# Two first gate blocks kept raw until the branch stage, other buffers for four weight loads, and a last gate pair in written order

## The chip, the cores and the metric

The program runs on one core of a Trainium2 chip. The metric is the time of one execution in microseconds of the device; lower is better. A core has a matrix engine (PE, with its weight loads shown apart as PEld), a vector engine (DVE), a scalar engine (ACT), a general engine (POOL), and a queue engine (SP) that issues transfers; ACT and POOL issue a few transfers of their own.

## The reference, cut to what matters

One encoder layer over 1024 tokens of width 1024: one input projection, two branches (neighbourhood attention and a gated linear recurrence), a gated merge, an output projection and an MLP. The change lies around the merge:

```python
(q_na, k_na, v_na, q_hg, z_f, z_b, i_hg, g_hg, gate_na, gate_hg) = split_cols(a @ w_in[l])
...
mix = jax.nn.sigmoid(gate_na) * y_na + jax.nn.sigmoid(gate_hg) * y_hg
h = h + mix @ w_o[l]
```

`y_na` and `y_hg` are the two branches' outputs after their own projections `w_na_out` and `w_hg_out`. The two gates have 2048 columns together; each is a product of the normalised input `a` with a slice of `w_in`.

## The kernel before, in words

Every matrix operand is float32 and is split into a high and a low part (`split`, lines 95 to 97: ACT casts the high part, DVE subtracts it from the source to get the low part). A product is three multiplies of 512 columns per 128 rows of depth: high by high, high by low, low by high. A `chain` (line 874) is such a product over half of the depth: 12 multiplies.

**Gates.** The gate columns are taken as 16 blocks of 128 columns in 8 pairs. The product of a pair with the input is done by a Winograd-like scheme with seven half products in place of eight. One of them, `g1[m]`, and the first half of the even block are computed early, in `first_gates` (line 903), two pairs at a time: four chains, then ACT copies the first product to `g1` (line 912) and takes the sigmoid of the second (`gate_out`, line 900) and writes it to DRAM (`gsp`, line 901). Those of pairs 0 to 3 are spread by the scheduler as filler through the last neighbourhood attention stage, which itself uses `Exp` on ACT (line 807), transposes on PE (lines 820 and 822, tile `ppt`), and on ACT and DVE takes the transposed scores apart again (lines 831 and 832, tile `PT`).

The rest is `gate_pair` (line 964), eight times. On PE, pair m issues the chains s4 (into bank `pc`), then the last chain of the pair before (a22, into that pair's `pb`), then s2 (into `pb`), s1 (adds into `pc`), s3 (adds into `pb`). DVE reads `pb` after s2 (line 972), `pc` after s1 (line 974), `pb` after s3 (line 977); POOL subtracts (line 978), DVE adds (line 979); the last chain's result is read at line 984. As s3 and a22 add into the bank that lines 972 and 977 read, PE may start s3 only when line 972 is done, and a22 only when line 977 is done. Weights of a pair come by two loads of 512 KB (line 953) into `raw` tiles, Winograd sums on DVE (lines 869 to 872) and five splits.

**Buffers.** `raw`, `hi` and `lo` tiles of 512 KB come from a pool `wp` with two buffers each; a second pool `gp` in the gate stage has two more of each. Pairs with odd m take `raw` from `wp`, even ones from `gp`.

**Branch stage** (line 1020 on). `branch_operand(br)` loads a branch's output from DRAM (`osp`) in four pieces of 512 KB (k = 0 to 3) through `raw` tiles of `wp`, and splits each piece into the operand tiles `o` (line 1018). For each pair of output columns the weights `w_hg` (then `w_na`) are loaded through the same two `raw` buffers (line 1025) and split; each product takes 12 multiplies (lines 122 to 124) into one of five banks, and DVE multiplies it by the gate `sg`, loaded from `gsp` (lines 1032, 1041, 1043, 1044).

**What sets the order.** The program is written in the order of the source and a list scheduler then reorders instructions on each engine as it expects them to be ready; each engine, and each queue, works through its list strictly in order. A stretch under `tc.manual_schedule` keeps the written order on the engines that it names.

Of the kernel before, what the change touches and what calls it, by code (L numbers as in the profile page):

```python
# [9 lines left out]
F32 = mybir.dt.float32  # L10
# [8 lines left out]
P = 128  # L19
# [29 lines left out]
def layer(ctx: ExitStack, tc: tile.TileContext, x, meta, w_in, w_na, w_hg, w_o, w_up, w_dn,  # L49
# [55 lines left out]
    def load_block(src, kc, scale=None, raw=None):  # L105

        if raw is None:
            raw = load_raw(src, kc)
        hi = wp.tile([P, KC, P], F32R, tag="hi", name="hi")
        lo = wp.tile([P, KC, P], F32R, tag="lo", name="lo")  # L110
        if scale is None:
            act.copy(hi[:, :kc], raw[:, :kc])  # L112
            dve.tensor_tensor(lo[:, :kc], raw[:, :kc], hi[:, :kc].bitcast(F32), op=ALU.subtract)  # L113
# [16 lines left out]
    def u_tiles(h, name):  # L130
        return [up.tile([P, KC, UW[h]], F32R, tag=f"u{h}{i}", name=f"{name}{h}{i}") for i in range(2)]
# [760 lines left out]
    def gate_col(c):  # L892
        return (C_GH if c < KC else C_GN) + (c % KC) * P
# [4 lines left out]
    def gate_out(c, h, t, src):  # L898

        act.activation(t, src, AF.Sigmoid)  # L900
        act.dma_start(gsp[c][:, h * TH:(h + 1) * TH], t)

    def first_gates(ms):

        blocks, ps = [], []
        for m in ms:
            hi, lo = load_block(w_in[:, gate_col(2 * m):gate_col(2 * m) + P], KC)
            blocks.append([[flat(t)[:, q * TH:(q + 1) * TH] for t in (hi, lo)] for q in range(2)])
        for m, b in zip(ms, blocks):
            ps.append(mm_tile())  # L910
            chain(ps[-1], b[0], aV["b11"], True)
            act.copy(g1[m], ps[-1])
        for m, b, p in zip(ms, blocks, ps):
            chain(p, b[1], aV["b21"], False)
            gate_out(2 * m, 0, gfp.tile([P, TH], F32, tag="go", name="go", bufs=2), p)

    psum_pools(pa=2, pb=2, pc=2)
    first_gates((0, 1))
# [27 lines left out]
    def gate_sums(m):  # L946

        raw = []
        for q in range(2):
            t = (wp.tile([P, KC, P], F32, tag="raw", name="raw") if m % 2 else  # L950
                 gp.tile([P, KC, P], F32, tag="raw", name="raw", bufs=2))
            c = gate_col(2 * m + q)
            sp.dma_start(t, w_in[:, c:c + P].rearrange("(k p) c -> p k c", p=P))
            raw.append(flat(t))
        sa, sb = g_tile("sx", D, bufs=2), g_tile("sx", D, bufs=2)
        winograd(dve, raw[0][:, :TH], raw[0][:, TH:], raw[1][:, :TH], raw[1][:, TH:],
                 sb[:, :TH], sa[:, TH:], sb[:, TH:], sa[:, :TH])
        W = {}
        W["s4"], W["s2"] = gate_weights(sa)
        W["s1"], W["s3"] = gate_weights(sb)  # L960
        W["a22"], = gate_weights(raw[1][:, TH:])
        return W

    def gate_pair(m, W, before):
        pb, pc = up_bank("pb"), up_bank("pc")
        p3 = gpr.tile([P, TH], F32, tag="p3", name="p3", bufs=2)
        chain(pc, W["s4"], aV["b22"], True)
        act.copy(p3, pc)
        before()
        chain(pb, W["s2"], aV["t2"], True)  # L970
        u1, u3, u2 = (g_tile("gv", TH, bufs=5) for _ in range(3))
        dve.tensor_tensor(u1, pb, g1[m], op=ALU.add)
        chain(pc, W["s1"], aV["t1"], False)
        dve.tensor_tensor(u1, u1, pc, op=ALU.add)
        gate_out(2 * m, 1, u1, u1)
        chain(pb, W["s3"], aV["t3"], False)
        dve.tensor_tensor(u3, pb, g1[m], op=ALU.add)
        pool.tensor_tensor(u3, u3, p3, op=ALU.subtract)
        dve.tensor_tensor(u3, u3, pc, op=ALU.add)
        gate_out(2 * m + 1, 1, u3, u3)  # L980

        def last():
            chain(pb, W["a22"], aV["t4"], False)
            dve.tensor_tensor(u2, pb, g1[m], op=ALU.add)
            gate_out(2 * m + 1, 0, u2, u2)
        return last

    first_gates((4, 5))
    first_gates((6, 7))
    W = gate_sums(0)  # L990
    for v in ("t2", "t1", "t3", "t4"):
        second_operand(v)
    last = lambda: None
    for m in range(NG):
        last = gate_pair(m, W, last)
        if m + 1 < NG:
            W = gate_sums(m + 1)
    last()
    gps.close()
    gfs.close()  # L1000

# [9 lines left out]
    osrc = [u_tiles(br, "o") for br in range(2)]  # L1011
    mix = [mixp.tile([P, KC, TH], F32, name=f"mix{h}") for h in (1, 0)][::-1]

    def branch_operand(br):
        for k in range(4):
            raw = wp.tile([P, KC, P], F32, tag="raw", name="raw")
            sp.dma_start(flat(raw), osp[br][k])
            split(*(t[:, 2 * k:2 * k + 2, :TH] for t in osrc[br]), raw.rearrange("p (h a) b -> p h (a b)", h=2))

    branch_operand(0)  # L1020
    for br, wsrc in enumerate((w_hg, w_na)):
        for jj in range(0, KC, 2):
            raw, hi, lo = (flat(wp.tile([P, KC, P], dt, tag=t, name=t))
                           for t, dt in (("raw", F32), ("hi", F32R), ("lo", F32R)))
            sp.dma_start(raw.rearrange("p (k c) -> p k c", k=4),
                         wsrc[:, jj * P:(jj + 2) * P].rearrange("(k p) c -> p k c", p=P))
            split(hi, lo, raw)
            if br == 0 and jj == 2:
                branch_operand(1)
            for j in (jj, jj + 1):  # L1030
                sg = sgp.tile([P, T], F32, tag="sg", name="sg")
                sp.dma_start(sg, gsp[8 * br + j])
                for h in range(2):
                    pm = mm_tile()
                    t = slice(h * TH, (h + 1) * TH)
                    for k in range(4):
                        c = slice(k * 2 * P + (j - jj) * P, k * 2 * P + (j - jj + 1) * P)
                        sh, sl = (o[:, 2 * k + h, :TH] for o in osrc[br])
                        mm3(pm, hi[:, c], lo[:, c], sh, sl, k == 0, k == 3)
                    if br == 0:  # L1040
                        dve.tensor_tensor(mix[h][:, j], pm, sg[:, t], op=ALU.mult)
# [608 lines left out]
```

## Time and profile before

| | |
|---|---|
| median of 3 runs | 1529.9 us (1528.22 to 1530.62) |
| the profiled execution, its own time | 1530.97 us |
| its span, first to last instruction | 1529.2 us (1.77 us lie around it) |
| PE busy | 1503.1 us, 98% of the span |
| DVE, ACT, POOL busy | 68%, 43%, 25% |
| mean granted PE clock | 0.997 |

A row of the timeline has the start in us, the duration in us, the engine, the source line, the operation, out<-in tiles, shape, and in brackets how long the engine sat idle before it and what ended that. A row of the waits has the engine and line that waited, who released it, and the total, the number of times and the longest. A row of the windows has, for a stretch of time, the busy time of each engine, and then the granted PE clock. Matmuls overlap: one of 512 columns lasts 0.39 us in its row, and the next starts 0.227 us behind it.

### The profile page before, as it was taken

To read this page: it belongs to the slowest core of one execution; us is meant where nothing else is said; L and a number is where in the kernel's file an instruction comes from. 1 tells how busy PE (TensorE), PEld (TensorE's weight loads), DVE (VectorE), ACT (ScalarE), POOL (GpSimd) and SP (SyncE) were. 2 spreads that over 40 slices of the span, in tenths; PEclk is the share of its full clock that TensorE was granted. 3 is DMA by queue.
4 is the path that set the end of the run, shared out by engine and by line. 5 is a ranking of instruction groups with operands and counts; after the bars stand their busy time and mean duration, and the time that the engine had idled before them with its cause. 6 is when DMAs were issued, how large, how long until landed. Compare 5 with 4: busy or idle time off the path is not lost.

```text
span 1529.2 us, 23532 instructions
## 1 busy us (share of the span) xinstructions
PE 1503.1 (98%) x9236; PEld 1255.8 (82%) x9236; DVE 1034.4 (68%) x1608; ACT 657.4 (43%) x1168; POOL 377.6 (25%) x355
## 2 busy tenths in 40 slices
PE   9999999999999999999999999999999999999998
PEld 8888888878888887887888887888888888888886
DVE  7876566645786777666475358877777544877876
ACT  6131313126665576334133235455555533434444
POOL 3313130324404400011000122444444200231142
PEclk9999999999999999999999999999999999999999
DMA  4201011113222227435756123544444576563324
GB/s 168 59 29 57 28 57 29 48 47 108 80 68 94 95 68 244 132 130 172 248 165 220 53 86 117 177 154 153 152 151 158 208 261 234 193 234 110 96 83 152
DMA packets 142591, 195.61 MB, mean 128 GB/s; under 512 B 8192, under 2 KB 90240, under 8 KB 142480
## 3 DMA queue, kind: packets, MB, share of 16 engines
q1 hardware_dynamic: 133216, 172.53, 34.3%
q10 hardware_dynamic: 7088, 14.24, 2.4%
q0 software_dynamic: 2176, 7.34, 1.3%
q8 instruction: 72, 1.18, 0.3%
q14 instruction: 39, 0.32, 0.1%
HBM read 139.56 MB, written 54.53 MB: 127 GB/s over the span
## 4 chain that ended last, share of the span: by engine, by line
PE 89%; DVE 5%; issue 2%; ACT 2%; DMA 1%; POOL 0%; POOLq 0%; ACTq 0%; SPq 0%; DVEq 0%
PE mm L122 11%; PE mm L123 10%; PE mm L124 10%; PE mm L1372 5%; PE pa L1372 4%; PE pb L879 4%; PE pb L880 4%; PE pb L881 4%; PE pb L1372 4%; PE pc L1372 4%; PE pc L879 3%; PE pc L881 3%; PE pc L880 3%; PE pa L879 2%; PE pa L880 2%
## 5 line engine op out<-in xcount | busy, mean ns | idle before, releaser
L122 PE MATMUL mm<-aT,hi 128*128 128x512 f32 (+2 forms) x600 | 214.7, 358 | 2.8 <-DVE QX L750 1.5
L124 PE MATMUL mm<-aT,lo 128*128 128x512 f32 (+2 forms) x600 | 212.2, 354 | 0.0
L123 PE MATMUL mm<-aT,hi 128*128 128x512 f32 (+2 forms) x600 | 211.2, 352 | 0.0
L97 DVE TENSOR_TENSOR dl<-ur,dh 128x1024 fp32r<-128x1024 f32 x54 | 71.1, 1316 | 87.3 <-ACT dh L96 85.3
L96 ACT CAST dh<-ur 128x1024 fp32r<-128x1024 f32 x54 | 56.9, 1054 | 166.4 <-issue 91.1
L122 PEld LDWEIGHTS mm<-aT,hi 128*128 128x128 f32 x600 | 113.2, 189 | 16.1 <-issue 1.7
L124 PEld LDWEIGHTS mm<-aT,lo 128*128 128x128 f32 x600 | 113.2, 189 | 12.5
L123 PEld LDWEIGHTS mm<-aT,hi 128*128 128x128 f32 x600 | 113.3, 189 | 11.7
L112 ACT CAST hi<-raw 128x1024 fp32r<-128x1024 f32 x34 | 35.7, 1051 | 97.1 <-PE mm L123 68.4
L1177 DVE TENSOR_TENSOR wl<-raw,wh 128x512 fp32r<-128x512 f32 x50 | 41.0, 822 | 36.4 <-ACT wh L1176 36.3
L1181 ACT ACTIVATE uv<-uv 128x512 f32<-128x512 f32 x48 | 30.4, 633 | 80.1 <-DVE uv L1289 48.9
L1177 DVE TENSOR_TENSOR wl<-sx,wh 128x512 fp32r<-128x512 f32 x70 | 61.1, 883 | 3.4 <-ACT wh L1176 3.3
L1176 ACT CAST wh<-sx 128x512 fp32r<-128x512 f32 x70 | 42.1, 619 | 42.2 <-PE pc L880 23.9
L1462 POOL TENSOR_TENSOR w<-w,tt 128x512 f32<-128x512 f32 x16 | 23.4, 1461 | 132.9 <-DVE tt L1461 113.2
L300 POOL TENSOR_TENSOR Y<-X,TN 128x512 f32<-128x512 f32 x20 | 34.3, 1713 | 84.7 <-DVE X L297 84.7
L805 DVE CUSTOM_DVE_ANT_0 pr<-nsc,NB 128x432 f32<-128x432 f32 (+1 forms) x64 | 35.2, 559 | 26.7 <-PE nsc L800 26.4
L113 DVE TENSOR_TENSOR lo<-raw,hi 128x1024 fp32r<-128x1024 f32 x34 | 46.1, 1357 | 8.5 <-ACT hi L112 8.4
L409 DVE TENSOR_TENSOR QQ<-QQ,TN 128x512 f32<-128x512 f32 x48 | 35.1, 741 | 22.9 <-PE sc L404 22.9
L879 PE MATMUL pb<-nt,wh 128*128 128x512 f32 x128 | 50.2, 392 | 0.4 <-DVE uv L1259 0.2
L122 PE MATMUL mm<-wh,mT 128*128 128x512 f32 x128 | 50.2, 392 | 0.0
L124 PE MATMUL mm<-wh,mT 128*128 128x512 f32 x128 | 50.0, 390 | 0.0
L880 PE MATMUL pb<-nt,wh 128*128 128x512 f32 x128 | 49.9, 390 | 0.0
(408 smaller groups left out, 4445.8 us busy)
## 6 DMA issues: line engine op xcount, KB each, us to landing
raw<-in_w_in SPq DMA_DIRECT2D x56, 512.0 KB, 4.1
ur<-usp SPq DMA_DIRECT2D x54, 512.0 KB, 3.6
raw<-in_w_up SPq DMA_DIRECT2D x16, 1024.0 KB, 6.1
usp<-us SPq DMA_DIRECT2D x60, 256.0 KB, 2.3
sg<-gsp SPq DMA_DIRECT2D x16, 512.0 KB, 4.0
w<-in_w_dn SPq DMA_DIRECT2D x16, 512.0 KB, 4.8
usp<-uv SPq DMA_DIRECT2D x30, 256.0 KB, 2.8
gsp<-gv ACTq DMA_DIRECT2D x24, 256.0 KB, 2.8
```

The source lines that it names most:

```text
L96: act.copy(hi, src)
L97: dve.tensor_tensor(lo, src, hi.bitcast(F32), op=ALU.subtract)
L113: dve.tensor_tensor(lo[:, :kc], raw[:, :kc], hi[:, :kc].bitcast(F32), op=ALU.subtract)
L122: pe.matmul(ps, lh, rh, start=first, stop=False)
L123: pe.matmul(ps, lh, rl, start=False, stop=False)
L124: pe.matmul(ps, ll, rh, start=False, stop=last)
L879: pe.matmul(ps, lhs[0][:, c], rhs[0][:, k], start=first and k == 0, stop=False, skip_group_check=True)
L880: pe.matmul(ps, lhs[0][:, c], rhs[1][:, k], start=False, stop=False, skip_group_check=True)
L881: pe.matmul(ps, lhs[1][:, c], rhs[0][:, k], start=False, stop=k == 3, skip_group_check=True)
L1176: act.copy(v(hi), src)
L1177: dve.tensor_tensor(v(lo), src, v(hi).bitcast(F32), op=ALU.subtract)
L1372: pe.matmul(ps, a[n == 2][:, q, j * P:(j + 1) * P], b[n == 1][:, q], start=first and n == 0, stop=last and n == 2, skip_group_check=True)
```

## The change

Three edits, with line numbers of the new file in the lists of order (lines after 916 are shifted: the old 972, 974, 977, 979 and 984 are 984, 987, 991, 993 and 999; the old 912 is 918; the old 1041 is 1067).

1. In `first_gates` the blocks of pairs 0 and 1 are stored to DRAM without the sigmoid (a copy in place of the activation, line 923), and the branch stage takes their sigmoid in place on the loaded gate (line 1058), for the first 512 columns of `gsp[0]` and `gsp[2]`.
2. The last call of `first_gates` (pairs 6 and 7) takes its weight tiles from `gp`, and even gate pairs take `raw` from `wp`, odd ones from `gp`.
3. The last gate pair is taken out of the loop. The first branch operand's four pieces are issued one by one between its chains, then the first branch weights, then the last chain; ACT and DVE keep this written order.

```diff
-    def first_gates(ms):
+    unsquashed = (0, 2)
+
+    def first_gates(ms, pool_=wp):
...
         for m in ms:
-            hi, lo = load_block(w_in[:, gate_col(2 * m):gate_col(2 * m) + P], KC)
+            raw, hi, lo = (pool_.tile([P, KC, P], dt, tag=t, name=t, bufs=2)
+                           for t, dt in (("raw", F32), ("hi", F32R), ("lo", F32R)))
+            c = gate_col(2 * m)
+            sp.dma_start(raw, w_in[:, c:c + P].rearrange("(k p) c -> p k c", p=P))
+            split(hi, lo, raw)
...
             chain(p, b[1], aV["b21"], False)
-            gate_out(2 * m, 0, gfp.tile([P, TH], F32, tag="go", name="go", bufs=2), p)
+            z = gfp.tile([P, TH], F32, tag="go", name="go", bufs=2)
+            if 2 * m in unsquashed:
+                act.copy(z, p)
+                act.dma_start(gsp[2 * m][:, :TH], z)
+            else:
+                gate_out(2 * m, 0, z, p)
...
-            t = (wp.tile([P, KC, P], F32, tag="raw", name="raw") if m % 2 else
+            t = (wp.tile([P, KC, P], F32, tag="raw", name="raw") if m % 2 == 0 else
                  gp.tile([P, KC, P], F32, tag="raw", name="raw", bufs=2))
...
-    def gate_pair(m, W, before):
+    def gate_pair(m, W, before, between=lambda n: None):
...
         before()
+        between(1)
         chain(pb, W["s2"], aV["t2"], True)
...
         dve.tensor_tensor(u1, pb, g1[m], op=ALU.add)
+        between(1)
         chain(pc, W["s1"], aV["t1"], False)
...
         gate_out(2 * m, 1, u1, u1)
+        between(1)
         chain(pb, W["s3"], aV["t3"], False)
...
         gate_out(2 * m + 1, 1, u3, u3)
+        between(1)
...
-    first_gates((6, 7))
+    first_gates((6, 7), gp)
...
+    def branch_operand(br):
+        osrc[br] = u_tiles(br, "o")
+        for k in range(4):
+            raw = wp.tile([P, KC, P], F32, tag="raw", name="raw")
+            sp.dma_start(flat(raw), osp[br][k])
+            split(*(t[:, 2 * k:2 * k + 2, :TH] for t in osrc[br]), raw.rearrange("p (h a) b -> p h (a b)", h=2))
+            yield
...
-    for m in range(NG):
+    for m in range(NG - 1):
         last = gate_pair(m, W, last)
-        if m + 1 < NG:
-            W = gate_sums(m + 1)
-    last()
+        W = gate_sums(m + 1)
+    operand = branch_operand(0)
+    with tc.manual_schedule(engines={act.engine, dve.engine}):
+        last = gate_pair(NG - 1, W, last, lambda n: next(operand))
+        ahead_w = [branch_weights(w_hg, 0)]
+        last()
...
+                if 8 * br + j in unsquashed:
+                    act.activation(sg[:, :TH], sg[:, :TH], AF.Sigmoid)
```

How the lists move. **ACT in the last attention stage**, before: the two sigmoids (`go`) each have a table load ahead of them, and the exponentials (`pr`) between them have one too; the last row is the cast that gives the transposed scores `PT` free.

```order
L900 ACT_TABLE_LOAD
L900 ACTIVATE go<-mm 128x512
L807 ACT_TABLE_LOAD
L807 ACTIVATE pr,sm<-pr,mn 128x432 x2
L831 CAST PT_6514<-ppt 128x2x128
L807 ACTIVATE pr,sm<-pr,mn 128x432
L807 ACTIVATE pr,sm<-pr,mn 128x288
L831 CAST PT_6514<-ppt 128x128
L901 DMA gsp_101<-go 128x512
L900 ACT_TABLE_LOAD
L900 ACTIVATE go<-mm 128x512
L831 CAST PT_6605<-ppt 128x4x128 x2
```

And the same place now, with copies at line 923:

```order
L923 COPY go<-mm 128x512
L807 ACTIVATE pr,sm<-pr,mn 128x432 x2
L831 CAST PT_6514<-ppt 128x2x128
L807 ACTIVATE pr,sm<-pr,mn 128x432
L807 ACTIVATE pr,sm<-pr,mn 128x288
L831 CAST PT_6514<-ppt 128x128
L924 DMA gsp_101<-go 128x512
L923 COPY go<-mm 128x512
L96 CAST hi<-raw 128x1024
L831 CAST PT_6605<-ppt 128x4x128
```

All three table loads are gone from here; one stands later, ahead of the first sigmoid of pair 2, after all exponentials. In the list of PE ten first-gate multiplies now stand between the transposes behind the attention product `pov` and the next ones; before, the two groups of transposes followed each other directly. In DVE's list the first Winograd sum of pair 0 (line 869) no longer stands between `low` and `PT` there.

**DVE at the hand-over from the gates to the branch stage**, before; `o_7876` is the low part of the first branch's operand, `gv<-pb,g_7` belongs to the last pair and `gv<-pb,g_6` to the pair before, and the two `lo<-raw` are weights, the second of them (128x1024) the first branch weights:

```order
L97 TENSOR_TENSOR o_7876<-raw,o_7875 128x2x512
L974 TENSOR_TENSOR gv<-gv,pc 128x512
L977 TENSOR_TENSOR gv<-pb,g_6_6667 128x512
L97 TENSOR_TENSOR lo<-raw,hi 128x512
L979 TENSOR_TENSOR gv<-gv,pc 128x512
L97 TENSOR_TENSOR o_7876<-raw,o_7875 128x2x512
L984 TENSOR_TENSOR gv<-pb,g_6_6667 128x512
L97 TENSOR_TENSOR o_7876<-raw,o_7875 128x2x512
L97 TENSOR_TENSOR lo<-raw,hi 128x1024
L972 TENSOR_TENSOR gv<-pb,g_7_6666 128x512
L974 TENSOR_TENSOR gv<-gv,pc 128x512
L977 TENSOR_TENSOR gv<-pb,g_7_6666 128x512
```

The same place now (the high parts on ACT stand in the same order):

```order
L999 TENSOR_TENSOR gv<-pb,g_6_6667 128x512
L97 TENSOR_TENSOR o_7791<-raw,o_7790 128x2x512
L984 TENSOR_TENSOR gv<-pb,g_7_6666 128x512
L97 TENSOR_TENSOR o_7791<-raw,o_7790 128x2x512
L987 TENSOR_TENSOR gv<-gv,pc 128x512
L97 TENSOR_TENSOR o_7791<-raw,o_7790 128x2x512
L991 TENSOR_TENSOR gv<-pb,g_7_6666 128x512
L993 TENSOR_TENSOR gv<-gv,pc 128x512
L97 TENSOR_TENSOR o_7791<-raw,o_7790 128x2x512
L97 TENSOR_TENSOR lo<-raw,hi 128x1024
L999 TENSOR_TENSOR gv<-pb,g_7_6666 128x512
```

All four operand pieces now stand behind the last result of pair 6 (line 999, the old 984); three of them stood ahead of it before. The first branch weights stood ahead of the last pair's first result and now stand behind all four pieces. The third piece stands ahead of line 991 (the old 977), on which the last chain waits.

**PE at the same place**, before: the last chain but one (`at_7030`, s3) ends, four branch multiplies follow, then the last chain (`at_7048`, a22).

```order
L881 MATMUL pb<-at_7030,lo 128x512
L122 MATMUL mm<-o_7875,hi 128x512
L123 MATMUL mm<-o_7876,hi 128x512
L124 MATMUL mm<-o_7875,lo 128x512
L122 MATMUL mm<-o_7875,hi 128x512
L879 MATMUL pb<-at_7048,hi 128x512
```

And now:

```order
L880 MATMUL pb<-at_7031,hi 128x512
L881 MATMUL pb<-at_7030,lo 128x512
L879 MATMUL pb<-at_7048,hi 128x512
L880 MATMUL pb<-at_7049,hi 128x512
L881 MATMUL pb<-at_7048,lo 128x512
```

The branch multiplies have all moved behind the last chain. In SP's list the loads of the four pieces come in order, the first ahead of the last gate weights, and the first branch weights right behind the fourth piece.

More of the change, by code (lines that the diff above doesn't have):

```diff
@@ L992, in layer, with branch_weights @@
         second_operand(v)
+    osrc = [None, None]
+    def branch_operand(br):
[5 more added lines that the diff above has]
+            yield
+    def branch_weights(wsrc, jj):
+        raw, hi, lo = (flat(wp.tile([P, KC, P], dt, tag=t, name=t))
+                       for t, dt in (("raw", F32), ("hi", F32R), ("lo", F32R)))
+        sp.dma_start(raw.rearrange("p (k c) -> p k c", k=4),
+                     wsrc[:, jj * P:(jj + 2) * P].rearrange("(k p) c -> p k c", p=P))
+        split(hi, lo, raw)
+        return hi, lo
     last = lambda: None
-    for m in range(NG):
+    for m in range(NG - 1):
         last = gate_pair(m, W, last)
-        if m + 1 < NG:
-            W = gate_sums(m + 1)
-    last()
+        W = gate_sums(m + 1)
[4 more added lines that the diff above has]
+        last()
     gps.close()
@@ L1009, in layer @@
     wrps = [wos.enter_context(tc.tile_pool(name=f"wrp{hc}", bufs=4, reuse_waits="tile")) for hc in range(2)]
-    osrc = [u_tiles(br, "o") for br in range(2)]
     mix = [mixp.tile([P, KC, TH], F32, name=f"mix{h}") for h in (1, 0)][::-1]
[L1014 to L1020, printed above, removed]
     for br, wsrc in enumerate((w_hg, w_na)):
         for jj in range(0, KC, 2):
[L1023 to L1027, printed above, removed]
+            hi, lo = ahead_w.pop() if ahead_w else branch_weights(wsrc, jj)
             if br == 0 and jj == 2:
-                branch_operand(1)
+                list(branch_operand(1))
             for j in (jj, jj + 1):
```

## The prediction

> **What bounds the kernel now.** The page comes first.
>
> ```profile
> span 1529.2 us, 23532 instructions
> PE 1503.1 (98%) x9236; PEld 1255.8 (82%) x9236; DVE 1034.4 (68%) x1608; ACT 657.4 (43%) x1168; POOL 377.6 (25%) x355
> ```
>
> PE is idle for 26 us out of 1529, and the change takes no multiply away. So it can only win or lose where PE waits, or where PE's clock falls. PE's waits, longest first, show which of these lie in the changed stretch (570 to 730 us):
>
> ```profile
> PE ppt L820 <- DVE PT L832: 2.4, 1, 2.4
> PE pb L879 <- DVE gv L972: 1.2, 1, 1.2
> PE mm L881 <- DVE lo L113: 0.5, 1, 0.5
> PE mm L879 <- ACT hi L112: 0.2, 1, 0.2
> ```
>
> Three places: the end of the attention stage, the last first-gate blocks, and the hand-over from the gates to the branch stage. I then cut the time around the first and the third into windows of 3.41 us, since the mean clock of 0.997 says that it fell somewhere (the number behind POOL's pair is the granted clock):
>
> ```profile
> 572.06:575.47 3.41, 1.10 (x9) 0.79 (x7) 2.67 (x5) 2.96 (x5) 0.00 (x0) 1.00 1.00 376
> 575.47:578.88 3.41, 3.37 (x12) 2.92 (x13) 3.09 (x5) 1.76 (x4) 0.00 (x0) 0.50 0.60 213
> 712.01:715.43 3.42, 2.50 (x12) 1.72 (x10) 1.72 (x3) 1.05 (x1) 0.00 (x0) 1.00 0.55 173
> 715.43:718.84 3.41, 3.15 (x14) 2.61 (x15) 0.98 (x3) 0.65 (x2) 0.00 (x0) 1.00 0.91 284
> ```
>
> Behind a stretch in which PE was busy for 1.10 of 3.41 us, the clock is 0.50 for the next 3.41 us; behind one with 2.50 busy it stays 1.00. So the first wait cost more than its 2.35 us: half of 3.41, or 1.7, goes on top.
>
> **Part 1: the raw gate blocks.** PE, ACT and DVE at the first place:
>
> ```profile
> 572.89 0.27 PE L822 MATMUL ppt<-ident,pr 128*128 128x128 f32 x1
> 575.51 0.88 PE L820 MATMUL ppt<-ident,pr 128*128 128x128 f32 x3 [2.35 <-DVE PT L832]
> ```
> ```profile
> 564.43 1.28 ACT L900 ACT_TABLE_LOAD   x1
> 566.34 1.28 ACT L807 ACT_TABLE_LOAD   x1
> 570.62 1.28 ACT L900 ACT_TABLE_LOAD   x1
> 571.91 0.60 ACT L900 ACTIVATE go<-mm 128x512 f32<-128x512 f32 x1
> 572.41 0.59 ACT L831 CAST PT<-ppt 128x512 fp32r<-128x512 f32 x1
> ```
> ```profile
> 572.76 0.69 DVE L847 COPY low<-pov 64x512 f32<-64x512 f32 x1 [1.56 <-PE pov L845]
> 573.38 0.68 DVE L869 TENSOR_TENSOR sx<-raw 128x512 f32<-128x512 f32 x1
> 574.09 0.68 DVE L849 TENSOR_TENSOR OT<-pov,low 64x512 f32<-64x512 f32 x1
> 574.70 1.27 DVE L832 TENSOR_TENSOR PT<-ppt,PT 128x512 fp32r<-128x512 f32 x2
> ```
>
> The third table load and its sigmoid hold the cast of `PT` until 572.41, and three DVE instructions (low, sx, OT) then stand ahead of the `PT` that frees the transpose bank. In the new order the loads are gone (3 x 1.28 us of ACT ahead of the cast), sx and OT no longer stand ahead of that `PT`, and ten multiplies of 0.227 us (2.3 us) stand on PE where it waited. Any two of these nearly cover 2.35 us, so I take the wait as gone, and the clock's fall with it: 2.35 + 1.7 = 4.0 us gained. The bounds are 0 (another bank wait of that length behind the moved multiplies) and 4.0; I sit at the upper end, as three changes point one way. The one table load that comes later stands among first-gate casts whose chains are 2.7 us long; up to 0.2 us, the wait quoted for `hi`.
>
> The two sigmoids that come back cost about 0.6 us of ACT each, as the row of 571.91. They lie in a stage where ACT has room and PE none:
>
> ```profile
> 740.00:770.00 30.00, 30.00 (x134) 24.82 (x134) 12.23 (x16) 3.75 (x4) 0.00 (x0) 1.00 0.55 177
> ```
>
> A gate half comes 0.6 us later to the DVE product that empties a bank; with five banks of 12 x 0.227 = 2.7 us each in turn, PE would see it only beyond some 13 us. Nothing; uncovered it would be 1.3 us.
>
> **Part 2: four weight tiles in other buffers.** The second place:
>
> ```profile
> 598.55 0.39 PE L881 MATMUL mm<-aT,lo 128*128 128x512 f32 x1
> 599.17 0.50 PE L879 MATMUL mm<-aT,hi 128*128 128x512 f32 x1 [0.23 <-ACT hi L112]
> 599.51 0.40 PE L880 MATMUL mm<-aT,hi 128*128 128x512 f32 x1
> 600.43 0.50 PE L881 MATMUL mm<-aT,lo 128*128 128x512 f32 x1 [0.53 <-DVE lo L113]
> ```
>
> From start to start PE loses 0.62 - 0.23 and 0.92 - 0.23, together 1.1 us. With buffers of their own these blocks need not wait for the pair before to give up `hi` and `lo`; I take 0.9 gained, between 0 and 1.1, leaving 0.2 for the later table load. The price is that pair 0's Winograd sums come later in DVE's list; there is room:
>
> ```profile
> 581.31 1.22 DVE L97 TENSOR_TENSOR lo<-sx,hi 128x1024 fp32r<-128x1024 f32 x1
> 610.99 0.39 PE L879 MATMUL pc<-aT,hi 128*128 128x512 f32 x1
> ```
>
> Pair 0's first weights were ready 28 us before their first chain. Nothing, and 0 to 1 us if that room were used up.
>
> **Part 3: the last pair in written order.** PE at the hand-over (end of s1, start and end of s3, start of the last chain, first branch multiply behind it):
>
> ```profile
> 714.12 0.39 PE L881 MATMUL pc<-at,lo 128*128 128x512 f32 x1
> 715.69 0.50 PE L879 MATMUL pb<-at,hi 128*128 128x512 f32 x1 [1.19 <-DVE gv L972]
> 718.33 0.39 PE L881 MATMUL pb<-at,lo 128*128 128x512 f32 x1
> 719.50 0.50 PE L879 MATMUL pb<-at,hi 128*128 128x512 f32 x1
> 722.37 0.39 PE L123 MATMUL mm<-o,hi 128*128 128x512 f32 x1
> ```
>
> By 722.37 four branch multiplies are done; they filled the gap in which DVE reads the bank behind s3. The durations for the new chain:
>
> ```profile
> 709.11 0.69 DVE L984 TENSOR_TENSOR gv<-pb,g 128x512 f32<-128x512 f32 x1 [1.05 <-PE pb L881]
> 710.75 0.63 ACT L900 ACTIVATE gv<-gv 128x512 f32<-128x512 f32 x1
> 708.05 0.59 ACT L968 COPY p<-pc 128x512 f32<-128x512 f32 x1 [0.45 <-ACT gv L900]
> L96 ACT CAST o<-raw x8: 1039/1052/1056, 693.8 to 732.6; 128x1024 fp32r<-128x1024 f32 x8
> L97 DVE TENSOR_TENSOR o<-raw,o x8: 1211/1226/2060, 694.9 to 733.7; 128x1024 fp32r<-128x1024 f32 x8
> DMA to landing us min/median/max: 3.3/3.7/7.6
> 704.49 1.29 POOL L978 TENSOR_TENSOR gv<-gv,p 128x512 f32<-128x512 f32 x1 [11.99 <-DVE gv L977]
> ```
>
> The landing row is that of the operand pieces (line 1017). In the new order ACT splits piece 0 only behind pair 6's last sigmoid. On the clock of this trace: pair 6's last sum is done at 709.11 + 0.69 = 709.8, its sigmoid at 710.5, its transfer is issued (0.45) by 710.9, piece 0 is cast by 712.0 and split by 713.2. Only then is a `raw` buffer free for piece 2, since pieces 0 and 1 hold both. Piece 2 lands 3.7 later, at 716.9, is cast by 718.0 and split by 719.2. DVE's read of the bank (the old line 977) stands behind that and is done at 719.9. Without its old wait s3 runs from 714.35 to 717.07 (12 x 0.227). So the last chain waits 717.07 to 719.95: **2.9 us**, in place of the 1.2 us ahead of s3, which goes.
>
> Next: POOL until 721.2 (1.29), DVE 721.9 (0.69), sigmoid 722.5, transfer issue 723.0. Behind these in ACT's list come piece 3 (cast by 724.0) and the branch weights' high part (725.1). PE ended the last chain at 719.95 + 2.72 = 722.7 and waits **2.4 us** more, as all branch multiplies now stand behind that chain. It does four with the high part (to 726.0), and waits **0.5 us** for the low part, which DVE has behind piece 3 (725.3) at 726.5. So four branch multiplies are done at 726.5 where it was 722.37: 4.2 us lost. Each restart adds 0.1 us (599.17 to 599.51 is 0.34, not 0.23) and there are two more: **4.4 us**. With the shortest landing it is 0.4 less, with 7.6 it is 3.9 more; I take the median. The branch weights are not late: their transfer starts at 719.2 and has until 724.0. SP's list now has piece 0's load ahead of the last gate weights, which it would hold up if its buffer came late; that buffer is given up with pair 6's sums, sooner than the one the gate weights need: nothing. POOL's list is as it was.
>
> **Sum.** -4.0 (first place) - 0.9 (second) + 4.4 (hand-over) = -0.5 us, on the profiled execution's 1530.97 us. That execution lies 1.07 above the median of the three runs, so I put the same difference on the median: 1529.9 - 0.5 = **1529.4 us**. A measurement of this kernel can tell about 0.2%, 3.1 us, from no change: faster is below 1526.8, slower above 1533.0.
>
> **Rivals.**
>
> *A, the forecast:* what the raw gates win is spent at the hand-over. For it speaks that the chain above is three lists in strict order. If the clock falls behind the 2.9 us wait, the last chain takes up to 1.7 us more, until 724.4, and the wait until 725.1 eats it. 1529.4 us.
>
> *B, the clock falls behind the second wait of the hand-over.* There it meets branch multiplies with nothing to hide them: 1.7 us more, 1531.1 us. For it: 2.4 us idle is as much as the 2.31 us that preceded the fall (3.41 - 1.10). Against it: the windows have fixed edges and the wait must lie in one, and a fall behind the first wait fills the second.
>
> *C, slower: the first place keeps its wait.* `low` still stands ahead of `PT` on DVE, and two splits of 1.2 us come close behind; if the transposes wait again for over 2 us, with the clock's fall, the 4.0 us are not won: 1533.4 us. [...] Against it: the ten multiplies moved into that very gap.
>
> *D, faster: the hand-over is free.* If piece 2 landed before 714, for instance because its buffer came free sooner than I read, the 1.2 us wait would go and nothing come: -4.0 - 0.9 - 1.2, 1523.8 us. Against it: two `raw` buffers, and the first is given up behind line 984's successor.
>
> *E, another rule for the clock.* If a wait of less than a window does not trip the clock, its fall at 575.47 came from something else and stays; then the first place wins 2.35 and the hand-over trips nothing: -2.35 - 0.9 + 4.4 = +1.15, 1531.1 us. Against it stands the order of the two windows above, 1.10 busy and then 0.50. [...]
>
> **How the numbers follow.** A 0.52, B 0.20, C 0.13, D 0.09, E 0.06. A, B and E lie within 0.2% of 1529.9: 0.78. C is slower: 0.13, D faster: 0.09. C and D are left out of the range. Its lower end gives back half of the hand-over's cost, 1529.4 - 2.2 = 1527.2. Its upper end is B on the assumption that the clock's fall at the first place was not in the median of the timed runs (they lie 2.4 us apart): 1531.1 + 1.7 = 1532.8.
>
> **What would show it.** Right: no table load beside the last exponentials, no wait over 0.5 us at the transposes before 585 us, granted clock 1.00 there; no wait at the last first-gate blocks; then at the last chain of pair 7 a PE wait of 2.5 to 3.5 us released by DVE's read behind s3, a second of about 2.4 us released by ACT's weight cast, a third of about 0.5 us, and piece 2 issued right behind the split of piece 0. Wrong: hand-over waits under 2 us together, a remaining wait on `PT`, or a half-clock window over branch multiplies (that is B).

## The result, and the profile after

| | before | after |
|---|---|---|
| median, us (runs) | 1530.02 (6) | 1538.83 (6) |
| lowest to highest | 1528.22 to 1531.83 | 1536.65 to 1540.54 |
| profiled execution, us | 1530.97 | 1539.47 |
| its span, us | 1529.2 | 1537.7 |

The ratio after to before is 1.0054, 95% interval 1.0044 to 1.0064: slower by about 8.3 us (0.0054 of 1530), and outside the forecast range. The head of the page after, as quoted of before:

```profile
span 1537.7 us, 23525 instructions
PE 1506.9 (98%) x9236; PEld 1257.4 (82%) x9236; DVE 1030.1 (67%) x1608; ACT 656.0 (43%) x1168; POOL 377.0 (25%) x355
```

The number of multiplies is the same; PE's waits are not. From the list of PE's waits after, those of the changed stretch:

```profile
PE mm L879 <- ACT g L918: 4.4, 1, 4.4
...
PE pb L879 <- DVE gv L991: 2.6, 1, 2.6
...
PE pov L836 <- ACT PT L831: 1.5, 1, 1.5
...
PE mm L124 <- DVE lo L97: 0.8, 2, 0.5
...
PE mm L122 <- ACT hi L96: 0.6, 1, 0.6
```

The wait of 2.35 us at the transposes, that of 0.53 at the last first-gate blocks and that of 1.19 ahead of s3 are gone. The longest one now, 4.4 us, is one that the forecast does not have.

To see where the 8.5 us between the two spans lie, I compare the start of the same multiplies in both timelines of PE: the first of the first-gate blocks, the first of gate pair 0, the last of s1 of pair 7, the last of the branch stage. Before (the second and third stand in the prediction):

```profile
540.38 0.40 PE L879 MATMUL mm<-aT,hi 128*128 128x512 f32 x1
...
808.28 0.39 PE L124 MATMUL mm<-o,lo 128*128 128x512 f32 x1
```

After:

```profile
539.94 0.40 PE L879 MATMUL mm<-aT,hi 128*128 128x512 f32 x1
...
613.97 0.39 PE L879 MATMUL pc<-aT,hi 128*128 128x512 f32 x1
...
717.10 0.39 PE L881 MATMUL pc<-at,lo 128*128 128x512 f32 x1
...
816.28 0.39 PE L124 MATMUL mm<-o,lo 128*128 128x512 f32 x1
```

| stretch | before, us | after, us | difference |
|---|---|---|---|
| up to the first first-gate multiply | 540.38 | 539.94 | -0.44 |
| end of attention and first-gate blocks | 70.61 | 74.03 | +3.42 |
| gate pairs, to the end of s1 of pair 7 | 103.13 | 103.13 | 0.00 |
| hand-over and branch stage | 94.16 | 99.18 | +5.02 |
| behind it, to the end of the span | 720.9 | 721.4 | +0.5 |

So two stretches carry it. The hand-over came out near its forecast of +4.4. The stretch ahead of it was forecast to win 4.9 and lost 3.4.

**The new wait.** PE, ACT, DVE and SP's queue after, around 590 to 606 us. PE first: the last multiply ahead of the wait, and the one behind it.

```profile
601.57 0.39 PE L881 MATMUL mm<-aT,lo 128*128 128x512 f32 x1
606.35 0.80 PE L879 MATMUL mm<-aT,hi 128*128 128x512 f32 x1 [4.39 <-ACT g L918]
```
```profile
588.88 2.18 ACT L96 CAST at<-gv 128x512 fp32r<-128x512 f32 x4
...
599.81 0.62 ACT L96 CAST at<-gv 128x512 fp32r<-128x512 f32 x1 [1.01 <-DMA gv<-tsp_t]
605.19 0.62 ACT L96 CAST at<-gv 128x512 fp32r<-128x512 f32 x1 [4.76 <-DMA gv<-tsp_t]
605.72 0.58 ACT L918 COPY g<-mm 128x512 f32<-128x512 f32 x1
```
```profile
593.62 0.69 DVE L869 TENSOR_TENSOR sx<-raw 128x512 f32<-128x512 f32 x1 [2.79 <-DMA raw<-in_w_in]
594.23 0.68 DVE L871 TENSOR_TENSOR sx<-raw 128x512 f32<-128x512 f32 x1
594.83 0.68 DVE L870 TENSOR_TENSOR sx<-sx,raw 128x512 f32<-128x512 f32 x1
595.43 0.68 DVE L97 TENSOR_TENSOR at<-gv,at 128x512 fp32r<-128x512 f32 x1
596.03 0.68 DVE L872 TENSOR_TENSOR sx<-raw,sx 128x512 f32<-128x512 f32 x1
596.63 2.49 DVE L97 TENSOR_TENSOR at<-gv,at 128x512 fp32r<-128x512 f32 x4
```
```profile
596.14 0.32 SPq L943 DMA_DIRECT2D gv<-tsp_t  x1
596.74 0.38 SPq L964 DMA_DIRECT2D raw<-in_w_in  x1
597.35 1.99 SPq L943 DMA_DIRECT2D gv<-tsp_t  x3
```

Read from the end. PE's chain for pair 6 needs the bank that ACT's copy to `g` empties. That copy took 0.58 us and its data had been there since 602; it stood on ACT behind the cast of the 14th operand piece of 16. The 14th piece was not loaded before 597.35, because its `gv` buffer (five in turn) was that of the 9th, which DVE split at 596.63. The 6th to 9th pieces had been cast by 591.1 (588.88 + 2.18). DVE split the 8th at 595.43 only, because pair 0's Winograd sums (`sx`) stood ahead of them in its list and waited until 593.62 for their weights' load. Before, the same 14th piece was issued 3.5 us sooner:

```profile
593.88 0.32 SPq L932 DMA_DIRECT2D gv<-tsp_t  x1
```

The transfer itself was slower too. From issue to landing the 14th piece took, after and before:

```profile
DMA to landing us min/median/max: 7.8/7.8/7.8
```
```profile
DMA to landing us min/median/max: 4.4/4.4/4.4
```

So it came 6.9 us later, half for the held buffer and half for the slower transfer; with either alone the wait would have been near 1 us (an estimate: 3.4 or 3.5 us off 4.39). When the buffers came free, the next weights and three pieces were issued within 2.2 us (596.74 to 598.95). That this bunching made the transfer slow was not tested by itself.

Before, those sums were done by 581 (the prediction's row of `lo<-sx`). In the other buffers, `wp`, their weights can only be loaded when the first-gate blocks of pairs 4 and 5 have given up the same tiles: after, these two loads are issued at 584.67 and 587.51, right behind the splits on DVE that end at 584.64 and 587.49.

**The clock.** Windows of 3.41 us after, on edges worked out from the fall of the clock behind the last multiply, at 1535.78 us (busy time of PE, PEld, DVE, ACT, POOL, then the granted clock):

```profile
600.52:603.94 3.42, 1.44 (x7) 0.86 (x5) 1.54 (x3) 0.00 (x0) 0.00 (x0) 1.00 0.93 326
603.94:607.35 3.41, 1.00 (x2) 0.83 (x3) 1.51 (x3) 2.16 (x5) 0.00 (x0) 0.50 0.59 188
607.35:610.76 3.41, 3.41 (x9) 2.64 (x8) 0.99 (x2) 0.47 (x1) 0.00 (x0) 0.50 0.00 1
719.99:723.40 3.41, 0.84 (x4) 0.53 (x4) 1.82 (x2) 0.88 (x1) 0.54 (x1) 1.00 0.59 196
723.40:726.81 3.41, 3.41 (x10) 2.64 (x9) 0.69 (x1) 1.52 (x2) 0.74 (x1) 0.50 0.98 343
```

The 4.39 us lie in two windows, with 1.44 and 1.00 us busy, and behind both the clock is 0.50. PE works at it from 606.35 to 610.76: its multiplies start 0.43 us apart there and 0.227 behind it. By an estimate from the two that costs half of 4.41, or 2.2 us. With that the first stretch nearly adds up: -2.35 -1.70 (old wait and clock), +1.51 (new wait at `pov`), -1.1 (old waits at the last blocks, from start to start), +4.39 +2.2, and 0.27 for a late start at 585.35 (0.50 behind the multiply before, where 0.23 is usual) make +3.2 of the +3.42.

**The hand-over.** PE, at the last chain of pair 7 and at the first branch multiplies:

```profile
722.78 0.50 PE L879 MATMUL pb<-at,hi 128*128 128x512 f32 x1 [2.57 <-DVE gv L991]
...
727.97 0.50 PE L122 MATMUL mm<-o,hi 128*128 128x512 f32 x1 [0.58 <-ACT hi L96]
...
729.41 0.50 PE L124 MATMUL mm<-o,lo 128*128 128x512 f32 x1 [0.25 <-DVE lo L97]
```

These are the three waits of the forecast in their order and with their releasers. The second is short because the last chain ran at clock 0.50 until 726.81.

### The profile page after: what moved, and what is told of

It is laid out like the page before. It is cut to its first block, busy times and chain, and to the rows that moved or that the text cites. A ratio compares the mean times of both kernels' runs of the same rounds, so it can differ in the third digit from the quotient of the medians.

```text
span 1537.7 us, 23525 instructions
## 1 busy us (share of the span) xinstructions
PE 1506.9 (98%) x9236; PEld 1257.4 (82%) x9236; DVE 1030.1 (67%) x1608; ACT 656.0 (43%) x1168; POOL 377.0 (25%) x355
## 4 chain that ended last, share of the span: by engine, by line
PE 44%; DVE 3%; DMA 2%; issue 2%; ACT 1%; POOL 0%; ACTq 0%; POOLq 0%; DVEq 0%
PE mm L1398 5%; PE pa L1398 4%; PE pb L1398 4%; PE pc L1398 4%; PE pb L879 3%; PE pb L880 3%; PE pb L881 3%; PE mm L124 2%; PE mm L123 2%; PE mm L122 2%; PE pc L880 2%; PE pc L879 2%; PE pc L881 2%; PE pa L880 2%; PE pa L881 2%
## 5 line engine op out<-in xcount | busy, mean ns | idle before, releaser
L112 ACT CAST hi<-raw 128x1024 fp32r<-128x1024 f32 x26 | 27.3, 1051 | 87.4 <-PE mm L123 67.0
L124 PE MATMUL mm<-o,lo 128*128 128x512 f32 x128 | 49.9, 391 | 0.8 <-DVE lo L97 0.8
L122 PE MATMUL mm<-o,hi 128*128 128x512 f32 x128 | 49.9, 390 | 0.6 <-ACT hi L96 0.6
L879 PE MATMUL pb<-nt,wh 128*128 128x512 f32 x128 | 50.2, 392 | 0.4 <-DVE uv L1285 0.2
```

The source lines that it names most:

```text
L122: pe.matmul(ps, lh, rh, start=first, stop=False)
L124: pe.matmul(ps, ll, rh, start=False, stop=last)
L879: pe.matmul(ps, lhs[0][:, c], rhs[0][:, k], start=first and k == 0, stop=False, skip_group_check=True)
```

## The experiments

Each was timed beside the kernel before; ratios are to it. Edits are shown against the changed kernel, and nothing of the computation is left out in any. Seven of the twelve also undo the written order of the last pair, in these lines, shown once:

```
-    for m in range(NG - 1):
+    for m in range(NG):
         last = gate_pair(m, W, last)
-        W = gate_sums(m + 1)
-    operand = branch_operand(0)
-    with tc.manual_schedule(engines={act.engine, dve.engine}):
-        last = gate_pair(NG - 1, W, last, lambda n: next(operand))
-        ahead_w = [branch_weights(w_hg, 0)]
-        last()
+        if m + 1 < NG:
+            W = gate_sums(m + 1)
+    last()
+    ahead_w = []
...
+    list(branch_operand(0))
     for br, wsrc in enumerate((w_hg, w_na)):
```

### Each part alone

**Raw blocks alone.** Old order of the last pair, and:

```
-            t = (wp.tile([P, KC, P], F32, tag="raw", name="raw") if m % 2 == 0 else
+            t = (wp.tile([P, KC, P], F32, tag="raw", name="raw") if m % 2 else
...
-    first_gates((6, 7), gp)
+    first_gates((6, 7))
```

> Of the three parts only the raw first-gate blocks are in. Theory T1 (the 4.39 us wait at the first-gate blocks of pairs 6 and 7, and the half clock behind it, come from the other buffers): none of that wait here; the 2.35 us wait at the transposes and its half clock are gone, a 1.5 us wait at the last pov may remain, so 2.5 to 4 us faster than before, ratio 0.9974 to 0.9984. Theory T2 (the raw blocks move the casts of the stage, and the wait comes from that): the 4 us wait is here, 4 to 8 us slower, ratio 1.003 to 1.005. Theory T3 (the written order of the last pair costs 8 us or more): as T1 here.

Measured: 1527.4 us, ratio 0.9986 (0.9977 to 0.9995), or -2.1 us. No wait over 0.53 us at the changed places, and the clock stays at 1.00. That is as T1 and T3 said, with a gain a little under their 2.5 us; T2 is out.

**Other buffers alone.** Old order of the last pair, and `unsquashed = ()`.

> Of the three parts only the other buffers are in. T1: a PE wait of 3 to 5 us at the last first-gate blocks, released by the copy to g behind a cast that waits for an operand piece, with the clock at half behind it; the wait at the transposes stays; 4 to 8 us slower than before, ratio 1.003 to 1.005. T2 and T3: within 1 us of before, ratio 0.9993 to 1.0007.

Measured: 1527.12 us, ratio 0.9979 (0.997 to 0.9988): faster by 3.2 us. T1 in this form falls: the buffers alone do not make the wait. None of the three theories had the gain. DVE's timeline shows why. In this kernel five operand pieces are split ahead of the sums, not three, and the 14th piece is issued at 594.12:

```profile
590.99 3.10 DVE L97 TENSOR_TENSOR at<-gv,at 128x512 fp32r<-128x512 f32 x5 [1.56 <-DMA gsp<-go]
595.18 0.69 DVE L869 TENSOR_TENSOR sx<-raw 128x512 f32<-128x512 f32 x1 [1.09 <-DMA raw<-in_w_in]
```
```profile
594.12 0.32 SPq L943 DMA_DIRECT2D gv<-tsp_t  x1
```

**Written order alone.** `unsquashed = ()`, and the two edits of "raw blocks alone" to the buffers.

> Of the three parts only the last pair's written order is in. T1: the hand-over costs what was forecast, waits of about 2.6 and up to 2.4 us in place of 1.2, so 3 to 5 us slower than before, ratio 1.002 to 1.0033; nothing new at the first-gate blocks. T3: 8 us or more slower, ratio above 1.005. T2: as T1 here.

Measured: 1536.17 us, ratio 1.0038 (1.0025 to 1.005), +5.8 us. PE waits 2.3 us at the last chain and 2.2 us for the weights' cast, as forecast (2.9 and 2.4), and 1.15 us, where it was 0.23, for the high part of a first-gate block. In this profile the second wait lies in one window, and branch multiplies then run at clock 0.50, from 722.91 to 726.33:

```profile
719.50:722.91 3.41, 1.23 (x6) 0.72 (x5) 1.36 (x2) 2.57 (x3) 0.00 (x0) 1.00 0.97 359
```

That is the fall of rival B, whose cost would be 4.4 + 1.7 = 6.1. In the trace, though, the hand-over stretch (711.91 to 811.12) lost 5.05 us, as much as in the whole change, where the fall lay elsewhere. The profiled execution, 1533.56 us, is the fastest of the five timed, so the rest of the 5.8 is not explained by it. T1's 3 to 5 is a little low, T3's 8 is out.

The three parts alone add up to -2.1 - 3.2 + 5.8 = +0.5 us. The whole change costs 8.3. Some 7.8 us, give or take about 3 by the four intervals, come only of parts together.

**The whole without the buffers.** The two edits of "raw blocks alone", last pair in written order.

> The changed kernel without the other buffers (raw blocks and written order stay). T1: no wait over 1 us at the first-gate blocks of pairs 6 and 7; raw blocks -2.5 to -4, hand-over +4.4: 0.5 to 2 us above before, ratio 1.0003 to 1.0013. T2: as the changed kernel, ratio 1.0054. T3: 4 to 6 us slower, ratio 1.003 to 1.004.

Measured: 1531.6 us, ratio 1.0015 (1.0006 to 1.0024), +2.3 us; 0.6 us is the longest wait at the first-gate blocks. It agrees with T1 but for a little. Without the buffers the excess is gone, so it needs them and one of the others.

### Which parts together

**Raw blocks and buffers.** Only the old order of the last pair.

> Raw blocks and other buffers together, the last pair in its old order. Alone they gave -2.1 and -3.2 us, so by their sum this would be 1525, ratio 0.9965. Theory T1b (raw blocks and other buffers together make the 4.39 us wait, since the g copy of pair 6 then stands on ACT behind the cast of an operand piece whose load came late): the wait and its half clock are here, -5.3 + 7.8, 2 to 3 us slower than before, ratio 1.001 to 1.002. Rival R1 (the wait needs the written order as well, which takes 4 more operand loads ahead or moves the branch loads): no such wait, 0.996 to 0.997.

Measured: 1530.15 us, ratio 1.0003 (0.9995 to 1.0012), where the sum of the two parts is 0.9965. The wait is there without the written order, so R1 is out:

```profile
PE mm L879 <- ACT g L918: 3.5, 1, 3.5
...
PE pov L836 <- ACT PT L831: 2.1, 1, 2.1
```

Together 5.6 us, which is what the two parts lose against their sum (0.0038 of 1530, 5.8 us). I had expected 2 to 3 us more, for half the clock behind it. In this execution the clock stayed:

```profile
601.19:604.60 3.41, 1.52 (x7) 0.94 (x5) 1.37 (x3) 0.00 (x0) 0.00 (x0) 1.00 0.92 327
604.60:608.02 3.42, 1.80 (x8) 1.50 (x9) 2.31 (x4) 2.63 (x5) 0.00 (x0) 1.00 0.51 156
```

The 3.5 us are split evenly over two windows, with 1.52 and 1.80 us busy, and from 608.02 on the clock is 1.00 too.

**The whole, with late weight loads.**

```
-    W = gate_sums(0)
     for v in ("t2", "t1", "t3", "t4"):
         second_operand(v)
+    W = gate_sums(0)
```

> The changed kernel, with pair 0's weight loads and sums written behind the second operands, so that they come later in the lists of SP, DVE and ACT. T1b with the cause in those loads and sums: operand pieces land sooner, the 4.39 us wait falls below 1 us and the clock stays; 5 to 8 us faster than the changed kernel, ratio to before 1.000 to 1.002. Rival R2 (the transfers themselves are too slow in this stretch, whatever the order): wait and time as in the changed kernel, ratio 1.0045 to 1.006.

Measured: 1532.76 us, ratio 1.0023 (1.0014 to 1.0032), 4.7 us less than the whole change. No PE wait at the first-gate blocks is left, and the clock stays at 1.00 there. The 14th piece is issued 6.4 us sooner than there, and lands 3.9 us behind its issue:

```profile
590.97 0.32 SPq L943 DMA_DIRECT2D gv<-tsp_t  x1
```

So the place of pair 0's loads and sums in the lists makes the wait, and R2, slow transfers whatever the order, is out: the transfer was slow in the changed kernel, but not with this order. The ratio is just above what T1b allowed.

**The whole, with the gate sums' raw tiles in their old buffers.** The first edit of "raw blocks alone"; the last first-gate blocks stay in `gp`.

> The changed kernel with the last first-gate blocks in their new buffers, but the raw tiles of the gate sums in their old ones (odd pairs in wp). Pair 0's sums then come ahead of the operand splits on DVE again. T1b, if the late sums of pair 0 are its cause: no wait over 1 us at the first-gate blocks; ratio 1.000 to 1.002. R2: as the changed kernel, 1.0045 to 1.006.

Measured: 1534.28 us, ratio 1.0034 (1.0021 to 1.0048). No wait at the first-gate blocks, as T1b says, but 1.8 us at `pov`, 2.6 at the last chain, and a ratio over the 1.002 expected. Of the two halves of the buffer edit it is the swap of the raw tiles that makes the 4.39 us wait; the time is not accounted for in full. The profiled execution, 1530.81 us, is the fastest of five and shows less of it than the median.

**Raw blocks and buffers, with late weight loads.** The edit of the late loads, and the old order of the last pair.

> Raw blocks and other buffers, old order of the last pair, and pair 0's weight loads and sums behind the second operands. T1b: the gains of the two parts add up and nothing takes them back: 1525 us, ratio 0.996 to 0.997. R2: the wait stays, ratio 1.001 to 1.002.

Measured: 1527.5 us, ratio 0.9983 (0.9974 to 0.9992), 2 to 3.5 us short of T1b, though the wait at the first-gate blocks is gone. The other wait of this kind has grown. ACT and PE at the end of the attention stage:

```profile
577.16 0.62 ACT L96 CAST aT<-gv 128x512 fp32r<-128x512 f32 x1 [3.77 <-DMA gv<-tsp_t]
577.68 0.26 ACT L831 CAST PT<-ppt 128x128 fp32r<-128x128 f32 x1
```
```profile
578.00 0.51 PE L836 MATMUL pov<-PT,Vn 128*128 128x512 f32 x1 [2.72 <-ACT PT L831]
```
```profile
576.09:579.50 3.41, 1.50 (x10) 1.38 (x11) 1.49 (x3) 2.34 (x6) 0.00 (x0) 1.00 0.93 316
579.50:582.91 3.41, 3.41 (x11) 2.73 (x10) 2.67 (x4) 0.49 (x1) 0.14 (x1) 0.50 0.79 233
```

A cast of 0.26 us on which PE waits stands behind one that waits 3.77 us for its load: 2.72 + 1.7 = 4.4 us.

### That order on ACT undone

**One raw block.** As the kernel just above, with `unsquashed = (0,)`. With it the list scheduler puts the last cast of `PT` ahead of the first cast of an operand piece.

> As the kernel with raw blocks and other buffers, old order of the last pair and late weight loads, which gave 0.9983 with a PE wait of 2.7 us at the last pov and half the clock behind it; here only the first of the two blocks is stored raw, and on ACT the last cast of PT then stands ahead of the first cast of an operand piece, not behind it. Theory T1c (a copy or cast that frees a PSUM bank stands on ACT behind a cast whose load is late; that alone makes these waits): the wait at pov is gone, about 4 us less than with two raw blocks if the clock stays too; the second block's sigmoid with its table loads may cost 1 to 2 us again; ratio 0.9955 to 0.9975. Rival R3 (the wait at pov comes from PE's or DVE's order): it stays over 2 us, ratio 0.998 to 0.999.

Measured: 1523.48 us, ratio 0.9962 (0.995 to 0.9975): by the ratios 3.2 us below the one with two raw blocks, as T1c says; R3 is out. (The lists of PE and DVE moved too; that ACT's order is the cause is read from the releaser of the wait above and its absence here.) PE's timeline shows no wait at all between 545 and 760 us. ACT at the place in question:

```profile
574.32 0.27 ACT L831 CAST PT<-ppt 128x128 fp32r<-128x128 f32 x1
574.47 0.64 ACT L96 CAST aT<-gv 128x512 fp32r<-128x512 f32 x1
```

This is the fastest version here, by the ratios 5.8 us below before and 14 below the changed kernel.

**No raw block.** As above, `unsquashed = ()`.

> Other buffers and late weight loads, old order of the last pair, and no block stored raw: the kernel with one raw block, which gave 0.9962, without that block. If the raw store is what takes the wait at the transposes away (theory T1c with the first part's gain real), that wait of about 1.8 us is back as with the other buffers alone: ratio 0.997 to 0.9985. If the buffers and the late loads did all of it (rival R4): no such wait, ratio 0.9955 to 0.9968.

Measured: 1526.38 us, ratio 0.9982 (0.9973 to 0.9991). The wait at the transposes is back with 1.75 us. So the raw store does earn its part, and R4 is out; the interval does not reach R4's.

**One raw block, gate sums' raw tiles in their old buffers.** `unsquashed = (0,)`, the first edit of "raw blocks alone", old order of the last pair.

> One raw block, the last first-gate blocks in their new buffers, the gate sums' raw tiles in their old ones, old order of the last pair. T1c: neither the wait at pov nor the one at the first-gate blocks, since on ACT no PT cast stands behind an operand's cast and the loads come as without the swap; ratio 0.9965 to 0.998. R3: a wait over 2 us at pov, ratio 0.998 to 1.000.

Measured: 1527.4 us, ratio 0.9989 (0.998 to 0.9998). The two waits in question are absent, as T1c says, but PE waits 1.64 us ahead of pair 7's s3 and 1.07 us for a first-gate `lo`, and the ratio is a miss. Each setting of buffers makes another list.

### The hand-over

**Read first.** The whole without the buffers, and in `gate_pair`:

```
-        between(1)
         chain(pb, W["s3"], aV["t3"], False)
         dve.tensor_tensor(u3, pb, g1[m], op=ALU.add)
+        between(1)
```

> As the changed kernel without the other buffers (1.0015), with DVE's read of the bank behind s3 put ahead of the split of operand piece 2 in the last pair's list. Hand-over theory H1 (that split, 1.23 us, holds the read): the PE wait at the last chain falls from 2.3 us to 0.8 to 1.1 and no longer halves the clock; the weights' cast comes about 1.2 us sooner, and the wait for it grows to about 2 us; 0 to 2 us faster than without the edit, ratio to before 1.0002 to 1.0015. Rival H2 (the load of piece 2 sets the wait): wait and ratio unchanged, 1.0015.

Measured: 1531.66 us, ratio 1.0021 (1.0012 to 1.003), no better than without the edit (1.0015). The wait at the last chain falls from 2.30 to 0.78 us, so H1 has the cause of that wait right, but its price is not saved:

```profile
720.37 0.63 PE L122 MATMUL mm<-o,hi 128*128 128x512 f32 x1 [3.02 <-ACT hi L96]
```

The wait for the weights' cast grows to 3.0 us, and a clock of 0.50 follows it, from 720.59 to 724.00, on branch multiplies. Counted from the last multiply of s1, DVE's read came 1.5 us sooner than without the edit, but POOL's subtract behind it took 2.15 us in place of 1.29; why was not tested. By the rows, what sets the start of the branch is the chain that follows: the last sum over POOL, its sigmoid, piece 3, then the weights. The edit mostly moved the place where PE waits for it.

## Why the prediction failed

**The step that failed** is in Part 2: "The price is that pair 0's Winograd sums come later in DVE's list; there is room", with the price "Nothing, and 0 to 1 us if that room were used up". The 28 us of room are those until pair 0's own chains, and they were indeed not used up: pair 0 starts without a wait. The price lay with what stands behind the sums. They went into DVE's list between the splits of the operand pieces, waited there for their own load, and held the splits, so the `gv` buffers, so SP's loads, so ACT's casts, so a copy that empties PE's bank; the load that was held came 6.9 us late, 3.4 of it because it also took 7.8 us to land, and PE waited 4.39 us. I followed the sums to their user and never asked who is queued behind them on DVE. The swap makes the load late (the wait goes where the raw tiles stay in their old buffers), and the raw blocks bring the sums forward among the splits (three splits ahead, where the buffers alone have five); neither does it alone. Why the scheduler places them so was only read from the lists, not tested.

**First place (-4.0).** The 2.35 us wait and its half clock went, as forecast. But the two bounds, 0 and 4.0, looked only at the transposes. The cast that feeds the next matmul stood behind an operand's cast and cost 1.51 us here and 2.72 in another kernel. The part alone gave -2.1 us (-0.8 to -3.5), about half the forecast. That fits a clock that did not fall behind the old wait in every execution (the mean granted clock of the runs before, timed beside this part, lies between 0.997 and 0.999), so that the 1.7 us were not there to be won in every one. No execution of the kernel before was profiled without that fall; the profile of the written order alone has the same wait of 2.35 us, split over two windows, at full clock:

```profile
573.91 0.52 PE L820 MATMUL ppt<-ident,pr 128*128 128x128 f32 x3 [2.35 <-DVE PT L832]
```
```profile
569.31:572.73 3.42, 2.25 (x16) 1.81 (x15) 1.83 (x5) 3.21 (x5) 0.00 (x0) 1.00 1.03 343
572.73:576.14 3.41, 2.23 (x14) 1.98 (x15) 3.41 (x6) 2.45 (x6) 0.00 (x0) 1.00 0.83 320
```

**Second place (-0.9).** The two old waits went. The buffers alone gave -3.2 us, more than that; but the list changed as a whole (the wait at the transposes was 1.76 us there, with the clock at 1.00 behind it, and the 1.19 us ahead of s3 was gone), so it is no proof of the term. Put in with the raw blocks, the same part cost 4.39 + 2.2.

**Hand-over (+4.4).** Right in mechanism and size. Piece 2 was issued at 716.46, behind the split of piece 0 that ended at 716.44. The stretch lost 5.02 us, of which 0.51 is a later wait for branch weights at 751.54: 4.5. Its clock fell to 0.50 behind the first wait, at 723.40, and most of that hid in the second, as rival A said. With the written order alone it fell behind the second, at 722.91, as rival B has it, but that stretch lost 5.05 us there: where the fall lay made hardly a difference.

**Rivals.** C had the right sign for a wrong reason: the first place did not keep its wait. None of them had a wait at the first-gate blocks. D is out. E, by which a wait shorter than a window does not trip the clock, is contradicted by the wait of 2.72 us above, behind which the clock was 0.50 from 579.50 to 582.91.

## What to carry to other kernels

When a change gives a step another buffer, look up who is queued behind that step on every engine that it visits, not only when its own result is needed: here a load that came late held its reader on DVE until 593.62, and with it a split whose operand had been cast by 591.1 and which ran at 595.43. On the engine that empties PSUM, look for a copy of half a microsecond behind a cast that waits for a transfer (0.58 us behind a wait of 4.76 here, and PE waited 4.39). And measure parts in pairs: here two parts that gain 2.1 and 3.2 us alone gain nothing together. What helped most was to move one pair's loads later and keep one raw block of the two.

## What the runs showed of the hardware

In these runs it depended on where a wait lay, more than on its length, whether PE's clock was halved behind it. In the changed stretch the clock stays at 0.50 for 3.41 us (before, 575.47 to 578.88) or twice that (after, 603.94 to 610.76), and the falls of one trace lie whole multiples of 3.413 us apart: before, 278 times from 575.47 to 1524.38; after, 35 times from 603.94 to 723.40 and 238 times from there to 1535.78. On edges found in this way I divided the traces of all runs, from 440 to 755 us, into windows of 3.41 us, and took those in which PE was busy for less than 2.3 us at full clock:

| run | window, us | PE busy, us | clock in the next window |
|---|---|---|---|
| read first | 717.17 to 720.59 | 0.40 | 0.50 |
| the whole change | 719.99 to 723.40 | 0.84 | 0.50 |
| the whole, with the gate sums' raw tiles in their old buffers | 710.86 to 714.28 | 0.86 | 0.50 |
| before | 572.06 to 575.47 | 1.10 | 0.50 |
| written order alone | 719.50 to 722.91 | 1.23 | 0.50 |
| the whole, with late weight loads | 712.70 to 716.12 | 1.26 | 0.50 |
| the whole without the buffers | 713.10 to 716.52 | 1.36 | 0.50 |
| the whole change | 600.52 to 603.94 | 1.44 | 0.50 |
| raw blocks and buffers, with late weight loads | 576.09 to 579.50 | 1.50 | 0.50 |
| raw blocks and buffers | 601.19 to 604.60 | 1.52 | 1.00 |
| other buffers alone | 572.93 to 576.34 | 1.65 | 1.00 |
| no raw block | 571.73 to 575.15 | 1.67 | 1.00 |
| one raw block, gate sums' raw tiles in their old buffers | 707.90 to 711.31 | 1.77 | 1.00 |
| the whole, with the gate sums' raw tiles in their old buffers | 574.33 to 577.74 | 1.78 | 1.00 |
| raw blocks and buffers | 604.60 to 608.02 | 1.80 | 1.00 |
| written order alone | 716.09 to 719.50 | 2.18 | 1.00 |
| written order alone | 572.73 to 576.14 | 2.23 | 1.00 |
| written order alone | 569.31 to 572.73 | 2.25 | 1.00 |
| the whole, with late weight loads | 572.76 to 576.17 | 2.25 | 1.00 |
| raw blocks and buffers | 577.30 to 580.71 | 2.27 | 1.00 |

Nine left a clock of 0.50 to the next window, with 0.40 to 1.50 us busy; eleven left 1.00, with 1.52 to 2.27 us. Where between 1.50 and 1.52 the two kinds part rests on one window of each; the next ones had 1.44 and 1.65 us. So a wait of 2.35 us halved the clock in one execution (before, 1.10 us busy in its window) and not in another (written order alone, 2.25 and 2.23 us in the two windows that it spans), and one of 3.5 us, split evenly over two, did not. A kernel with one such wait can differ by up to 1.7 us from one execution to the next for that alone, an estimate: half of one window of 3.41 us at a clock of 0.50.
